# An instruction order for four engines, worked out in the kernel's source by an account of times, in the recurrence stage of a two-layer encoder

## The chip, the core and the metric

The kernel runs on one core of a Trainium2 chip. The metric is the device time of one execution in microseconds (us). A core has the engines PE (matrix products), DVE (VectorE), ACT (ScalarE) and POOL (GpSimd); SP issues most of the DMA loads. Each engine takes its instructions in the order in which the program holds them, and an instruction that waits for something holds up those behind it on the same engine. PEclk in a view is the clock that was granted to PE, as a share of full speed.

## The reference

Two layers over one sequence of 256 tokens of width 1024, all in fp32. Each layer has a token mixer and a mixture of experts, and each of these is modulated by shift, scale and gate rows that come from a conditioning vector `c`:

```python
for i in range(DEPTH):                               # DEPTH = 2
    mod = silu_c @ ada_w[i] + ada_b[i]
    sh_t, sc_t, ga_t, sh_c, sc_c, ga_c = jnp.split(mod, N_MOD, axis=-1)
    hn = modulate(rms_norm(x, norm_tm_g[i]), sh_t, sc_t)
    tm = rwkv7_mix(hn, ...) if i % 2 == 0 else dilated_attention_mix(hn, ...)
    x = x + ga_t[:, None, :] * tm
    hn = modulate(rms_norm(x, norm_cm_g[i]), sh_c, sc_c)
    x = x + ga_c[:, None, :] * hier_moe(hn, ...)
```

`rwkv7_mix` of layer 0 is a bidirectional delta-rule recurrence: `S_t = S_{t-1}(diag(w_t) + a_t^T b_t) + v_t^T k_t`, `y_t = S_t r_t`, for 16 heads of 64 and both directions, with low-rank projections for decay, rate and output gate, a norm over each head and an output product `o @ w_o`. `hier_moe` picks one of 4 groups and two of its 8 experts for each token; all 32 experts have weights to load.

## The kernel before, in words

The program has these stages in a row: the modulations that layer 0's mixer needs, the recurrence stage (65 to 451 us of the profiled execution), the choice of the experts, the experts of layer 0, the attention, the experts of layer 1.

**The recurrence stage** works on 8 pairs of heads. A pair i goes through: `project(i)` (products `kr` and `v` from 1 MB and 640 KB of weights, then `rates`), `scale_keys` and `chunks` (products `G`, `BT`, `R2`, done when `("ready", i)` is), `inverse(i)` (a chain of small fp16 products `iv`, each of which waits for a copy on ACT or DVE of the one before), `recur(i)` (four steps of products `R`, `U`, `S`, `Y`) and `finish(i)` (norm, transposition `yT`, gate, sum into `oT[:, i]`). `finish_last` ends pair 7: its last instruction writes `oT<-gsq,sT`, and it is called the last finish here. The output product `wo` goes over `oT` in two halves: 16 matmuls over pairs 0 to 3 (`out_first`), then 16 over pairs 4 to 7 (`out_second`), and its sums are added to `x`.

**The modulation flow.** Beside all this `modulation_flow` sums six more modulation rows (gate, shift and scale that the experts of layer 0 and the mixer of layer 1 need). Each row is a product of `silu(c)` with 1024 x 1024 weights, made on DVE: 8 chunks of 512 KB come by DMA into `aring`, two buffers, and each is multiplied and added to `acc` in two instructions of 512 columns. After the eighth chunk of a row, PE sums over partitions (tile `ada`), and DVE makes columns of it (`modc`, `nsh`, `nsc`). So there are 48 chunks and 96 adds. When all are done the flow marks `("ada", 0)`.

**What waits for `("ada", 0)`.** The generator `releases` gives the memory of the stage back part by part, each time followed by `later(n)`, which opens more buffers for the weights stream `wring`. Its first line is `yield after(("project", 7), ("ada", 0))`. Until then `wring` has two buffers. The router of the experts (`start_router`) waits for `("ada", 0)` too: its bias `lb` is a product with the modulation's shift.

**The weights stream.** All weights of the program come over one queue, SP, in a fixed plan: `kr` and `vl` (the `v` weights) of the 8 pairs, four loads `rwo` of 1 MB for `wo`, 96 of 1 MB for the experts of layer 0 (`wring<-in_w_moe_dram`), then those of the attention (`qkv`) and of layer 1's experts. The `rwo` weights are multiplied by the gate row on POOL before use. The `aring` loads stand on the same queue.

**What sets the order.** The function `weave` runs the generators of the stage, one step of one generator at a time. A step records its instructions, and a generator yields how many microseconds it would rest, or what it waits for (`after(...)`). In the kernel before, `weave` counts the PE work recorded so far as its clock, and takes among the ripe generators the one with the lowest `RANK`. PE's instructions then keep the order of recording; those of DVE, ACT, POOL and SP are ordered by a scheduler with the priority that `weave` sets from its clock and `OFFSET`:

```python
            ripe = [s for s in free if s[2] <= now]
            s = min(ripe, key=lambda v: RANK[v[1]]) if ripe else min(free, key=lambda v: v[2])
...
            tc.cur_priority = base + int(20 * max(0.0, 10 + now + OFFSET[s[1]]))
            r = next(s[0], "end")
```

PE's result banks are the pools `pp`, `ps`, `iv` and `ch`, two each. In `modulation_flow` a chunk is followed by `yield PACE` (4.0), and a whole row by 5.0 more.

## Time and profile before

| | us |
|---|---|
| median of three timed executions | 1194.64 |
| lowest and highest of them | 1184.44, 1194.68 |
| the profiled execution's own time | 1175.46 |
| its span in the trace | 1173.7 |
| PE busy in the span | 1031.4 (88%) |
| DVE busy | 620.2 (53%) |
| ACT busy | 431.6 (37%) |
| POOL busy | 149.7 (13%) |
| HBM read, mean over the span | 319.22 MB, 273 GB/s with what is written |

Busy time is the time in which an engine worked on an instruction; the shares are means over stages that differ much, so a stage is read by its own window. The profiled execution is below the timed ones; a difference worked out in its times is put on the median as it is.

### The profile page before, as it was taken

To read this page: it belongs to the slowest core of one execution; us is meant where nothing else is said; L and a number is where in the kernel's file an instruction comes from. 1 tells how busy PE (TensorE), PEld (TensorE's weight loads), DVE (VectorE), ACT (ScalarE), POOL (GpSimd) and SP (SyncE) were. 2 spreads that over 40 slices of the span, in tenths; PEclk is the share of its full clock that TensorE was granted. 3 is DMA by queue.
4 is the path that set the end of the run, shared out by engine and by line. 5 is a ranking of instruction groups with operands and counts; after the bars stand their busy time and mean duration, and the time that the engine had idled before them with its cause. 6 is when DMAs were issued, how large, how long until landed. Compare 5 with 4: busy or idle time off the path is not lost. (4 is left out here: it accounts for less than half of the span.)

```text
span 1173.7 us, 25024 instructions
## 1 busy us (share of the span) xinstructions
PE 1031.4 (88%) x10580; PEld 675.4 (58%) x10580; DVE 620.2 (53%) x1460; ACT 431.6 (37%) x913; POOL 149.7 (13%) x110
## 2 busy tenths in 40 slices
PE   7789889999988998978987899898979999789886
PEld 2666667766766555434442388687868754344422
DVE  4774678478585446212211367999984752121112
ACT  2544455455446342101000366656544621010012
POOL 1020010010012600000000012122472000000000
PEclk9789999899979999989998999999989999899999
DMA  9462524325243676998999987887745589999995
GB/s 366 179 237 77 181 77 151 109 95 168 74 131 129 269 288 251 388 418 358 421 420 421 420 358 266 310 303 275 282 145 171 209 339 409 413 370 421 420 422 234
DMA packets 53197, 322.01 MB, mean 274 GB/s; under 512 B 5922, under 2 KB 6562, under 8 KB 21458
## 3 DMA queue, kind: packets, MB, share of 16 engines
q1 hardware_dynamic: 51986, 315.88, 69.0%
q0 software_dynamic: 800, 3.36, 0.7%
q8 instruction: 87, 1.43, 0.5%
q10 hardware_dynamic: 288, 1.05, 0.3%
q14 instruction: 36, 0.29, 0.1%
HBM read 319.22 MB, written 1.05 MB: 273 GB/s over the span
## 5 line engine op out<-in xcount | busy, mean ns | idle before, releaser
L271 PE MATMUL gu<-wring,xT 128*32 128x512 f32 x1024 | 132.6, 616 | 16.8 <-PEq L1609 10.2
L376 DVE SCALAR_TENSOR_TENSOR acc<-aring,silu,acc 128x512 f32<-128x512 f32 x140 | 116.0, 860 | 17.5 <-DMA aring<-in_w_ada_dram 17.3
L467 POOL TENSOR_TENSOR wl<-wring,wh 128x1024 f16<-128x1024 f32 x24 | 57.0, 2377 | 403.4 <-ACT wh L466 400.9
L271 PE MATMUL qkv<-hh,wh 128*128 128x256 f16 x384 | 106.1, 276 | 1.8 <-ACT hh L1761 1.8
L271 PE MATMUL qkv<-hl,wh 128*128 128x256 f16 x384 | 105.7, 276 | 1.8 <-DVE hl L1762 1.8
L271 PE MATMUL qkv<-hh,wl 128*128 128x256 f16 x384 | 106.0, 276 | 1.2 <-DVE wl L473 1.2
L271 PEld LDWEIGHTS gu<-wring,xT 128*32 128x32 f32 x1024 | 30.8, 112 | 100.5 <-issue 82.0
L271 PEld LDWEIGHTS <-wh 128*128 128x128 f16 x768 | 76.1, 99 | 12.8 <-issue 3.5
L271 PE MATMUL dn<-wring,hidT 128*32 128x256 f32 x1024 | 65.5, 404 | 18.4 <-ACT hidT L1564 18.4
L473 DVE SCALAR_TENSOR_TENSOR wl<-wring,wh 128x1024 f16<-128x1024 f32 x56 | 70.5, 1264 | 16.4 <-ACT wh L469 16.3
L271 PE MATMUL acc<-y,back 128*128 128x512 f32 (+1 forms) x144 | 66.0, 581 | 10.3 <-DVE y L1591 8.1
L271 PEld LDWEIGHTS xT<-oh,x 128*128 128x128 f32 x512 | 59.0, 192 | 21.1 <-issue 9.2
L469 ACT ACTIVATE wh<-wring 128x1024 f16<-128x1024 f32 x56 | 58.6, 1050 | 33.0 <-PE qkv L271 23.2
L1366 DVE SCALAR_TENSOR_TENSOR sg<-sg,gu 128x256 f32<-128x256 f32 x16 | 6.7, 420 | 116.8 <-ACT sg L1365 116.8
L1591 DVE TENSOR_TENSOR y<-dn,ga 128x512 f32<-128x512 f32 x28 | 19.4, 692 | 88.3 <-PE dn L271 56.7
L271 PE MATMUL xT<-oh,x 128*128 128x128 f32 x512 | 63.5, 280 | 2.5 <-DVE oh L1475 2.5
L1365 ACT ACTIVATE sg<-gu 128x256 f32<-128x256 f32 x16 | 6.1, 384 | 145.6 <-PE gu L271 145.6
L271 PEld LDWEIGHTS dn<-wring,hidT 128*32 128x32 f32 x1024 | 31.9, 115 | 48.2 <-ACT hidT L1564 22.3
L1507 ACT ACTIVATE back<-bT 128x256 f32<-128x256 f32 x16 | 6.2, 386 | 131.0 <-PE acc L271 131.0
L271 PE MATMUL qkv<-wh,hh 128*128 128x256 f16 x192 | 52.3, 273 | 0.0
L271 PE MATMUL qkv<-wh,hl 128*128 128x256 f16 x192 | 52.3, 273 | 0.0
L271 PE MATMUL qkv<-wl,hh 128*128 128x256 f16 x192 | 52.3, 273 | 0.0
(355 smaller groups left out, 2090.4 us busy)
## 6 DMA issues: line engine op xcount, KB each, us to landing
wring<-in_w_moe_dram SPq DMA_DIRECT2D x192, 1024.0 KB, 19.8
aring<-in_w_ada_dram SPq DMA_DIRECT2D x96, 512.0 KB, 4.6
wring<-in_w_qkv_dram SPq DMA_DIRECT2D x36, 1024.0 KB, 8.4
wring<-in_w_kr_dram SPq DMA_DIRECT2D x8, 1024.0 KB, 5.9
wring<-in_w_vl_dram SPq DMA_DIRECT2D x8, 640.0 KB, 5.0
wring<-in_w_rwo_dram SPq DMA_DIRECT2D x4, 1024.0 KB, 8.1
wring<-in_w_ato_dram SPq DMA_DIRECT2D x4, 1024.0 KB, 6.6
x<-in_x_dram POOLq DMA_DIRECT2D x2, 512.0 KB, 7.2
```

The source lines that it names most:

```text
L271: return on_pe(nc.tensor.matmul(out=o, lhsT=lhsT, rhs=rhs, start=start, stop=stop, **kw))
L376: V.scalar_tensor_tensor(out=acc[:, s], in0=w[:, s], scalar=silu[:, k:k + 1], in1=acc[:, s], op0=ALU.mult, op1=ALU.add)
L467: eng.tensor_tensor(out=lo, in0=src, in1=hi, op=ALU.subtract)
L469: A.activation(out=hi, in_=src, func=AF.Copy, scale=by)
L473: V.scalar_tensor_tensor(out=lo, in0=src, scalar=by, in1=hi, op0=ALU.mult, op1=ALU.subtract)
L1365: A.activation(out=o, in_=ps[:, 0:256], func=AF.Tanh, scale=0.5)
L1366: V.scalar_tensor_tensor(out=o, in0=o, scalar=1.0, in1=ps[:, 0:256], op0=ALU.add, op1=ALU.mult)
L1507: A.activation(out=back, in_=ps[:, 0:S], func=AF.Copy)
L1591: V.tensor_tensor(out=y, in0=py[c], in1=gates[i, 5][:, c * 512:(c + 1) * 512], op=ALU.mult)
```

## The change

The order of the recurrence stage is now made in the source for PE, DVE, ACT and POOL. `account` keeps for each engine the time at which it is free, and for each tile when it was written and read; prices are in `COST` (a fixed part and one by element) and in `mm`, `HAND` is what a hand-over from one engine to another takes. An `Engine` wrapper around DVE, ACT and POOL prices each instruction and keeps it in program order. A generator now yields the engine of its next step and the tiles or bank pools that the step needs; `weave` works out when each live generator's next step could start, adds the stream's `GIVE_WAY`, and takes the smallest.

The steps are cut finer for this (a yield ahead of nearly each instruction), and some are moved: the results `Y` of the recurrence have a generator of their own (`results`) and a bank pool of their own (`ch=1, yy=1` in place of `ch=2`), `inverse(i)` waits for `("matrices", i)`, which is marked earlier than `("ready", i)`, `hidden_gate` runs as a generator of its own, two mixes of the token shift (`xv`, `xg`) are made by DVE and ACT step by step. The products are fp32 as before. `modulation_flow` has two accumulators of 512 columns, its adds are on DVE as before, and in the account a chunk's adds start no earlier than 6.0 after the end of the adds of the chunk before.

```diff
-RANK = dict(X=0, C=1, R=2, F=3, D=4, G=5, S=6, H=6, W=7, A=2.5)
-OFFSET = dict(X=0, C=-6, R=-4, F=-2, D=-2, G=-1, S=0, H=0, W=0, A=8)
+GIVE_WAY = dict(X=0, C=0, R=0, D=0.1, Y=0.2, F=0.3, G=0, K=0, S=0.1, B=0.3, H=0, W=0.5, A=0.3)
+
+COST = dict(V=(0.16, 0.00105), A=(0.19, 0.0008), P=(0.15, 0.00217))
+HAND = dict(T=0.3, V=0.15, A=0.15, P=0.15)
+SWITCH = 0.1
...
+    def account(e, t, outs, ins):
+
+        start = free[e]
+        for n in ins:
+            w = wrote.get(n)
+            if w:
+                start = max(start, w[0] + (0.0 if w[1] == e else HAND[w[1]]))
+        for n in outs:
+            w = wrote.get(n)
+            if w and w[1] != e:
+                start = max(start, w[0] + HAND[w[1]])
+        free[e] = end = start + t
+        for n in outs:
+            wrote[n] = (end, e)
+        for n in ins:
+            read[n] = max(end, read.get(n, 0.0))
+        step_end[0] = max(step_end[0], end + HAND[e])
+
...
+                        account(self.e, 0.1, [], [])
+                    else:
+                        a, b = COST[self.e]
+                        n = max(int(np.prod(v.shape[1:])) for v in outs)
...
-
-        return tc.keep_in_program_order(i) if pinned[0] else i
+            psum_n.pop()
+
+    def on_pe(i, o, a, b, t):
+        if pinned[0]:
+            tc.keep_in_program_order(i)
+            k = (a.shape[0] <= 64, int(np.prod(a.shape[1:])) <= 64, b.dtype)
+            if k != kind[0]:
+                t += SWITCH * (2 if b.dtype == F32 else 1)
+            kind[0] = k
+            account("T", t, [o.tensor.name], [a.tensor.name, b.tensor.name])
+        return i
...
     def weave(*streams):
 
 
-        live = [[g, n, 0.0, None] for g, n in streams]
+
+
+        live = [[g, n, 0.0, ("T", ())] for g, n in streams]
         base, now, pinned[0] = tc.cur_priority, 0.0, True
+        for t in (free, wrote, read, slots):
...
+            e, deps = s[3]
+            t = free[e]
+            for d in deps:
+                if isinstance(d, str):
+                    d = released(d)
+                    if d is None:
+                        return None
+                elif d is True:
+                    d = s[2]
+                elif not isinstance(d, float):
+                    w = wrote.get(d.tensor.name, (0.0, e))
+                    d = w[0] + (0.0 if w[1] == e else HAND[w[1]])
+                t = max(t, d)
+            return t
+
         while live:
+            best = None
...
-            free = [s for s in live if not s[3]]
-            assert free, [s[1] for s in live]
-            ripe = [s for s in free if s[2] <= now]
-            s = min(ripe, key=lambda v: RANK[v[1]]) if ripe else min(free, key=lambda v: v[2])
-            now = max(now, s[2])
-            before = pe_work[0]
-            tc.cur_priority = base + int(20 * max(0.0, 10 + now + OFFSET[s[1]]))
+                if callable(s[3]):
+                    if not s[3]():
+                        continue
+                    s[2], s[3] = max(s[2], now), ("T", ())
+                t = start_of(s)
+                if t is None:
+                    continue
+                v = t + GIVE_WAY[s[1]] - (SWITCH if s is last and s[3][0] == "T" else 0.0)
+                if best is None or v < best[0]:
+                    best = (v, t, s)
+            assert best, (now, [(s[1], s[3]) for s in live], {k: [(n, wrote.get(n), read.get(n)) for n in v[-3:]] for k, v in slots.items()})
+            _, now, s = best
+            step_end[0] = now
+            tc.cur_priority = base + int(20 * now)
             r = next(s[0], "end")
+            last = s
             if r == "end":
                 live.remove(s)
                 continue
-            used = pe_work[0] - before
-            now += used + (0.12 if used else 0.0)
...
-        ctx2.enter_context(banks(pp=2, ps=2, iv=2, ch=2))
+        ctx2.enter_context(banks(pp=2, ps=2, iv=2, ch=1, yy=1))
...
         def modulation_flow():
 
-            for i, m, k in ADA_RWKV:
+            taken = 0.0
+            for n, (i, m, k) in enumerate(ADA_RWKV):
                 w = modulations.take((i, m, k))
                 if k == 0:
-                    acc = modulations.pools[0][0].tile([128, D], F32, name="acc", tag="acc", bufs=1)
-                ada_add(acc, w, k, k == 0)
...
+                    g = gates[i, m] = const.tile([128, D], F32, name=f"ga{m}", tag=f"ga{m}", bufs=1)
+                    P.dma_start(out=g, in_=ap["p_adab"][i:i + 1, m * D:(m + 1) * D].to_broadcast([128, D]))
+                for e in range(2):
+                    yield ("V", taken + 6.0, PACE * n + 4.0)
+                    a, v = acc[e], w[:, e * 512:e * 512 + 512]
+                    if k == 0:
+                        V.tensor_scalar(out=a, in0=v, scalar1=silu[:, k:k + 1], scalar2=None, op0=ALU.mult)
+                    else:
+                        V.scalar_tensor_tensor(out=a, in0=v, scalar=silu[:, k:k + 1], in1=a, op0=ALU.mult, op1=ALU.add)
...
-        streams = dict(X=releases(), C=recurrences(), R=inverses(), F=finishes(), D=readies(), G=last_gates(),
-                       S=supply(), W=outputs(), A=modulation_flow())
+        streams = dict(X=releases(), C=recurrences(), R=inverses(), D=readies(), Y=results(), F=finishes(),
+                       G=last_gates(), S=supply(), B=hidden_gate(), W=outputs(), A=modulation_flow())
```

**Place 1: DVE around the last finish.** `oT<-gsq,sT` is the last finish, `acc` are the sums of the modulations, `x_64` and `x_65` the two halves of `x`. In the program before:

```order
L1187 TENSOR_TENSOR YT<-YT,rsy 128x2x128
L1194 TENSOR_TENSOR gsq<-yT,g_5961 128x256
L1195 TENSOR_TENSOR oT<-gsq,sT 128x256
L596 SCALAR_TENSOR_TENSOR x_64<-wo,x_64 128x512 x2
L596 SCALAR_TENSOR_TENSOR x_65<-wo,x_65 128x512 x2
L565 COPY zT<-zT 128x4x128
L496 TENSOR_REDUCE nss<-sums 128x2
```

In the changed program, from the same instruction on:

```order
L306 TENSOR_TENSOR gsq<-yT,g_6113 128x256
L306 TENSOR_TENSOR oT<-gsq,sT 128x256
L306 SCALAR_TENSOR_TENSOR acc_6143<-aring,silu,acc_6143 128x512
L306 SCALAR_TENSOR_TENSOR acc_6144<-aring,silu,acc_6144 128x512
L306 SCALAR_TENSOR_TENSOR acc_6143<-aring,silu,acc_6143 128x512
```

and behind these, when the pair of `acc` adds has stood there four times:

```order
L306 TENSOR_TENSOR modc<-ada,cols 128x8
L306 TENSOR_SCALAR nsh<-modc 128x8
L306 SCALAR_TENSOR_TENSOR x_64<-wo,x_64 128x512 x2
L306 TENSOR_SCALAR acc_6621<-aring,silu 128x512
L306 TENSOR_SCALAR acc_6622<-aring,silu 128x512
L306 SCALAR_TENSOR_TENSOR x_65<-wo,x_65 128x512
L306 SCALAR_TENSOR_TENSOR acc_6621<-aring,silu,acc_6621 128x512
L306 SCALAR_TENSOR_TENSOR acc_6622<-aring,silu,acc_6622 128x512
L306 SCALAR_TENSOR_TENSOR x_65<-wo,x_65 128x512
```

Before, no add into `acc` stands behind the last finish. In the changed program 24 of the 96 adds do, those of the last 12 chunks: four chunks of one row, then the eight of the next row, among which stand the adds of `wo` to `x` and the chain `nss` that makes the norm of `x`.

**Place 2: PE at the same point.** The last `yT` is what the last finish reads. Before:

```order
L271 MATMUL wo<-wring,oT 128x512 x4
L275 MATMUL yT<-cst,YT 128x128 x2
L271 MATMUL wo<-wring,oT 128x512 x5
L275 MATMUL zT<-cst,x_64 128x128 x8
L275 MATMUL zT<-cst,x_65 128x128 x4
L271 MATMUL lg<-rws,zT 128x36
L275 MATMUL zT<-cst,x_65 128x128 x4
```

Changed:

```order
L348 MATMUL wo<-wring,oT 128x512 x4
L352 MATMUL yT<-cst,YT 128x128 x2
L348 MATMUL wo<-wring,oT 128x512 x12
L348 MATMUL ada<-cst,acc_6143 128x1 x4
L348 MATMUL ada<-cst,acc_6144 128x1 x4
L348 MATMUL wo<-wring,oT 128x512 x4
L348 MATMUL ada<-cst,acc_6621 128x1 x4
L348 MATMUL ada<-cst,acc_6622 128x1 x4
L348 MATMUL lb<-rw_72,modc 1x36 x8
```

Behind the last `yT` there were 5 `wo` matmuls; now there are 16, with 16 `ada` and 8 `lb` among and behind them, ahead of the transpositions `zT` that the router starts from. The first 16 `wo` now end with the four ahead of `yT`. In the whole stage PE changes the kind of its work (tile shape or type of the weights) 373 times in place of 395, counted in the two orders.

**Place 3: SP from the last loads of `v` weights on.** Before:

```order
L153 DMA wring<-in_w_vl_dram 128x1280
L153 DMA aring<-in_w_ada_dram 128x1024 x4
L153 DMA wring<-in_w_kr_dram 128x2048
L153 DMA aring<-in_w_ada_dram 128x1024 x4
L153 DMA wring<-in_w_vl_dram 128x1280
L153 DMA aring<-in_w_ada_dram 128x1024 x2
L153 DMA wring<-in_w_rwo_dram 128x2048 x4
L153 DMA wring<-in_w_moe_dram 128x2048 x45
```

Changed, from the second `rwo` group on (the `aring` rows that follow alternate in the same way with `moe` rows up to 41 of the latter in a row):

```order
L156 DMA wring<-in_w_rwo_dram 128x2048
L156 DMA aring<-in_w_ada_dram 128x1024 x2
L156 DMA wring<-in_w_rwo_dram 128x2048
L156 DMA aring<-in_w_ada_dram 128x1024 x5
L156 DMA wring<-in_w_rwo_dram 128x2048
L156 DMA aring<-in_w_ada_dram 128x1024 x3
L156 DMA wring<-in_w_rwo_dram 128x2048
L156 DMA aring<-in_w_ada_dram 128x1024 x2
L156 DMA wring<-in_w_moe_dram 128x2048
L156 DMA aring<-in_w_ada_dram 128x1024 x2
L156 DMA wring<-in_w_moe_dram 128x2048
```

Before, all 48 loads into `aring` stood ahead of the first `rwo`, and the 96 expert loads of layer 0 followed with no `aring` between them. In the changed program 10 `aring` loads stand behind the fourth `rwo`, and only 4 expert loads ahead of the last `aring`; the fourth `rwo` takes the `wring` buffer of the second, which is read by the second 8 of the first 16 `wo`.

## Rows read from the trace of the kernel before

**Rows 1.** Busy time by engine in the recurrence stage and the first experts.
```profile
core 0: us, PE busy (x) PEld busy (x) DVE busy (x) ACT busy (x) POOL busy (x), PEclk, DMA share, GB/s
65.00:450.00 385.00, 349.86 (x5187) 255.63 (x5188) 244.88 (x631) 184.68 (x415) 56.88 (x46) 0.94 0.43 150
...
469.00:667.00 198.00, 171.69 (x1384) 76.74 (x1384) 40.33 (x99) 23.28 (x68) 0.00 (x0) 0.96 0.98 405
```

**Rows 2.** What PE waited for in 65 to 450 us: total, times, longest.
```profile
PE kr L271 <- ACT at L806: 4.9, 3, 1.7
PE R L271 <- DVE SD L1099: 4.3, 6, 1.1
PE yT L275 <- DVE rsq L352: 3.5, 2, 2.9
```

**Rows 3.** Two windows inside the recurrence stage, columns as in rows 1.
```profile
215.00:225.00 10.00, 10.00 (x86) 7.94 (x87) 4.65 (x13) 1.68 (x5) 0.00 (x0) 0.60 0.34 105
320.00:340.00 20.00, 16.66 (x189) 11.89 (x190) 15.19 (x43) 9.53 (x19) 2.43 (x2) 0.57 0.53 163
```

**Rows 4.** A window inside the first experts, columns as in rows 1.
```profile
560.00:580.00 20.00, 18.52 (x162) 8.92 (x163) 4.87 (x11) 2.55 (x7) 0.00 (x0) 1.00 1.01 421
```

**Rows 5.** SP's queue in time: start, length, loads in a row.
```profile
360.80 14.06 SPq L153 DMA_DIRECT2D wring<-in_w_rwo_dram  x4
374.90 87.04 SPq L153 DMA_DIRECT2D wring<-in_w_moe_dram  x22
...
596.05 47.55 SPq L153 DMA_DIRECT2D wring<-in_w_moe_dram  x20
```

**Rows 6.** The page's DMA issues: count, KB, median us to landing.
```profile
wring<-in_w_moe_dram SPq DMA_DIRECT2D x192, 1024.0 KB, 19.8
```

**Rows 7.** DMA issues of 60 to 360 us, as in rows 6.
```profile
aring<-in_w_ada_dram SPq DMA_DIRECT2D x44, 512.0 KB, 3.9
wring<-in_w_kr_dram SPq DMA_DIRECT2D x7, 1024.0 KB, 5.9
```

**Rows 8.** DVE in time: the last sums, the last finish, the first output sum.
```profile
347.55 2.07 DVE L376 SCALAR_TENSOR_TENSOR acc<-aring,silu,acc 128x512 f32<-128x512 f32 x3
...
450.82 0.42 DVE L1195 TENSOR_TENSOR oT<-gsq,sT 128x256 f32<-128x256 f32 x1
452.46 0.69 DVE L596 SCALAR_TENSOR_TENSOR x<-wo,x 128x512 f32<-128x512 f32 x1 [1.22 <-PE wo L271]
```

**Rows 9.** PE in time around the last finish (two records are one matmul).
```profile
449.92 0.41 PE L275 MATMUL yT<-cst,YT 128*128 128x128 f32 x2 [0.26 <-DVE YT L1187]
450.16 4.84 PE L271 MATMUL wo<-wring,oT 128*128 128x512 f32 x10
```

**Rows 10.** PE's groups in 65 to 450 us: records, busy, mean ns.
```profile
L271 PE MATMUL wo<-wring,oT 128*128 128x512 f32 x54 | 29.5, 645 | 1.8 <-DVE x L596 1.8
L271 PE MATMUL ada<-cst,acc 128*128 128x1 f32 x64 | 9.8, 283 | 0.0
L271 PE MATMUL lb<-rw,modc 128*1 128x36 f32 x16 | 0.7, 197 | 0.0
```

**Rows 11.** PE in time, `kr` matmuls alone between other kinds.
```profile
86.08 1.03 PE L271 MATMUL kr<-xk,wring 128*128 128x256 f32 x4
86.95 0.60 PE L275 MATMUL BT<-cst,BK 128*128 128x128 f32 x4
...
113.41 1.13 PE L271 MATMUL kr<-xk,wring 128*128 128x256 f32 x4
114.47 0.44 PE L271 MATMUL iv<-Q,X 64*64 64x64 f16 x16
```

**Rows 12.** DVE's sums of the modulations in 65 to 450 us, as in rows 10.
```profile
L376 DVE SCALAR_TENSOR_TENSOR acc<-aring,silu,acc 128x512 f32<-128x512 f32 x79 | 61.0, 792 | 14.2 <-DMA aring<-in_w_ada_dram 14.1
L374 DVE TENSOR_SCALAR acc<-aring,silu 128x512 f32<-128x512 f32 x10 | 4.6, 481 | 0.0
```

**Rows 13.** POOL's gating of the output weights in 65 to 450 us.
```profile
L590 POOL TENSOR_TENSOR wring<-wring,ga 128x512 f32<-128x512 f32 x16 | 20.2, 1291 | 12.9 <-PE R L271 12.9
```

More of the change, by code (lines that the diff above doesn't have):

```diff
@@ new lines, in trunk, with __init__, __getattr__, call @@
+    class Engine:
+        def __init__(self, e, nc_engine):
+            self.e, self.nc_engine = e, nc_engine
+        def __getattr__(self, name):
+            f = getattr(self.nc_engine, name)
+            def call(*args, **kw):
+                i = f(*args, **kw)
+                if pinned[0]:
+                    tc.keep_in_program_order(i)
+                    aps = [(k, v) for k, v in itertools.chain(enumerate(args), kw.items()) if hasattr(v, "tensor")]
+                    outs = [v for k, v in aps if k in ("out", "accum_out", 0)]
+                    ins = [v for k, v in aps if k not in ("out", "accum_out", 0)]
+                    if name == "dma_start":
+                        account(self.e, 0.1, [], [])
+                    else:
+                        a, b = COST[self.e]
+                        n = max(int(np.prod(v.shape[1:])) for v in outs)
+                        account(self.e, a + b * n, [v.tensor.name for v in outs], [v.tensor.name for v in ins])
+                return i
+            return call
@@ L787, in keys, with first_keys @@
             ws[i] = dict(sq=sq, kT=krT[:, 0], rT=krT[:, 1])
+        def first_keys():
+            kr = stream.take(("kr", 0)).rearrange("p (j k n) -> p j k n", j=2, k=KD)
+            ps = bank(name="kr", tag="pp")
+            for j, xs in enumerate((xk, xr)):
+                for _ in product(ps[:, j * S:(j + 1) * S], kr[:, j], xs):
+                    pass
+            keyed(0, ps, 1.0)
         def rates(i, w):
+            yield ("T", w["sq"], "pp")
             ps = bank(name="ss", tag="pp")
@@ L1173, in finish_last @@
         def finish_last(w):
-            yield after(("half", 7), ("gates", 0), ("finish", 6))
+            yield after(("early", 7), ("gates", 0), ("finish", 6))
             y4 = w["YT"].rearrange("p z a n -> p (z a) n")
@@ L1235, in out_first @@
         def out_first():
-            yield after(("project", 7), ("finish", 3), ("gate", 2))
             for c in range(2):
-                w = gated(stream.take(("rwo", 0, c)), gates[0, 2][:, c * 512:(c + 1) * 512], 4)
-                yield 6.0
+                w = stream.take(("rwo", 0, c))
+                yield from gating(w, gates[0, 2][:, c * 512:(c + 1) * 512], 4)
                 for t in range(NTT):
+                    yield ("T", w, oT, "pp")
                     ps = bank(name="wo", tag="pp")
@@ L1266, in outputs @@
+            for w in two:
+                yield from gating(w, gates[0, 2], 2)
+                blocks2.append(w.rearrange("p (k n) -> p k n", k=2))
+            yield after(("inverse", 7), ("finish", 5), ("finish", 6))
             for t in range(NTT):
                 for c in range(2):
+                    yield ("T", "iv" if c else "ps")
                     po[t, c] = bank(name="wo", tag="iv" if c else "ps")
-            yield from out_second(po, (4, 5), blocks[0])
-            yield after(("finish", 6))
@@ L1271, in outputs @@
-            yield 1.0
-            yield from out_second(po, (6,), last_rows[0])
-        last_rows = []
-        for _ in keys(0):
-            pass
+                    wrote.pop(po[t, c].tensor.name)
+            yield from out_second((4, 5, 6))
+        first_keys()
         hidden()
-        ws[0].update(vl=stream.take(("vl", 0)), wait=0.0)
+        vls[0] = stream.take(("vl", 0))
         for _ in rates(0, ws[0]):
             pass
-        done.add(("rates", 0))
-        xv = kept(2, "xv")
@@ L1312, in finishes @@
             for i in range(7):
-                yield after(("recur", i))
+                yield after(("outputs", i))
                 yield from finish(i, ws[i])
-            yield after(("half", 7))
+            yield after(("early", 7))
             yield from finish_last(ws[7])
@@ L1319, in start_router @@
             yield after(("ada", 0), ("recur", 6))
-            yield from router.start()
+            yield ("T", "pp")
+            for _ in router.start():
+                yield ("T", True)
         def releases():
```

471 lines of the change are left out of this document (302 added, 169 removed).

## The prediction

> **What bounds the kernel now.** I read the busy times by stage first. In the recurrence stage PE works 349.86 of 385 us and is the busiest engine by far, so only 35.1 us there are idle [rows 1]; the reader is to see that no order can take the stage below its PE work. In the first experts PE works 171.69 of 198 us, but the DMA share is 0.98 [rows 1], and a window in the middle has 1.01 and 421 GB/s [rows 4]: there the weights come no faster. 1 MB (1.0486 million bytes) at 421 GB/s is 2.49 us, while PE takes 171.69/96 = 1.79 us for what 1 MB brings. So the end of the first experts is set by when their loads start and how many are in by the time the experts begin. Then I read the queue of the loads: the four `rwo` loads start at 360.80, expert loads follow at 374.90 without a gap in the plan, 22 of them by 461.9, and the last is issued at 596.05 + 47.55 = 643.6 [rows 5]. With 19.8 us to landing [rows 6] it is in at 663.4. The last finish ends at 450.82 + 0.42 = 451.2 [rows 8]; I call this time F, and F' the same event in the changed program. So in the kernel before the expert weights are complete at F + 212.
>
> The stage and the loads have to be summed apart, because the change touches both, and in opposite directions.
>
> **Part 1: the order of the stage, F' against F.** Three terms make the last finish earlier.
>
> First, PE work that moves behind it. Behind the last `yT` stood 5 `wo` matmuls, now 16 (place 2). A record group of 54 is 27 matmuls in 29.5 us, so 1.09 us each [rows 10]: 11 x 1.09 = 12.0 us. 16 `ada` matmuls at 9.8/32 = 0.306 us are 4.9 us, and eight `lb`, half of 0.7 us and a little, about 1 us [rows 10]. Together 18 us no longer stand ahead of F'. This isn't a gain of the kernel, it is only later; it returns in part 2.
>
> Second, 22 fewer changes of kind on PE. The price of one is bounded by two places. A group of two `kr` matmuls between `BT` transpositions is followed 0.87 us after its start, the same group between `iv` products after 1.06 us [rows 11]. So a change costs 0 to about 0.2 us; I take 0.1, the middle, 2 us in all.
>
> Third, idle time. The waits that an account of the hand-overs can see coming are those in which PE's fixed order put a product at the head too early: `kr` for the copies of `rates` (4.9), `yT` for the norm chain (3.5) [rows 2]. I take these two, 8 us, as what the order saves: in the middle of the stage there is always another product to put there. `R` waits for `SD` inside the recurrence itself (4.3, six times) [rows 2]; at the end of the stage, where pair 7 has no pair behind it, nothing can fill that, so I leave it. The bounds: 6 us of idle more, when pinned DVE and ACT queues make the longest wait (2.9) [rows 2] come twice again, and 30 us less, when nearly all of the 35.1 vanishes.
>
> The clock is a fourth, which I set at nothing. In 215 to 225 and 320 to 340 us the granted clock was 0.60 and 0.57 while PE was busy in 10.0 of 10 and 16.66 of 20 us [rows 3], the lower of its two levels for most of that time. At full clock these 30 us would have taken 10 x 0.40 + 20 x 0.43 = 12.6 us less. The first window shows the low clock under full load, so nothing in these rows says that another order would avoid it.
>
> Sum: F' = F - (18 + 2 + 8) = F - 28. Bounds of this gain: 18 + 0 - 6 = 12, and 18 + 2 + 30 + 12.6 = 63.
>
> DVE gets 32 instructions for the two mixes and many small pinned ones; it is busy in 245 of 385 us [rows 1], so I cost them at nothing as long as the order lets them run beside PE's 350. If that cover is gone they are in the lower bound.
>
> **Part 2: the tail behind F'.** DVE holds 24 adds of the modulations behind the last finish (place 1), and SP holds 10 `aring` loads behind the fourth `rwo` (place 3). Before, the last adds ran at 347.55 to 349.6 [rows 8], 100 us ahead of the last finish. Followed step by step:
>
> The fourth `rwo` waits for the buffer that the second 8 `wo` read; these end just ahead of the last `yT`, and `yT` starts 1.3 us before F [rows 8, 9]. So it is issued at F' - 1.5. A 1 MB load landed after 5.9 us in this stage [rows 7]: F' + 4.4. POOL multiplies it in four pieces of 1.29 us [rows 13]: F' + 9.6. The 8 `wo` that don't need it are done by then, four that do run until F' + 14, and `ada` until F' + 16.4. Meanwhile chunks 38 and 39 have landed and are summed (two adds of 0.79 a chunk, 1.6 us) [rows 12], and 40 and 41 load into the two buffers. The last four `wo` end at F' + 20.8. DVE's order puts two sums into `x` (0.69 each [rows 8]) ahead of chunk 40, the other two and the norm chain ahead of chunk 42. So chunk 40 is summed at about F' + 21, 41 at F' + 23, and the adds of 42 start at about F' + 25. From here two buffers turn: a buffer that is freed is loaded 3.9 us later [rows 7], so two chunks take 3.9 + 1.6, about 5.5 us. The loads of 42 and 43 have been issued when 40 and 41 were summed, so they wait for DVE; chunks 42 to 43 end at F' + 28, 44 to 45 at F' + 34, 46 to 47 at F' + 39. The last `aring` load is issued when 45 is summed, at F' + 34.
>
> Behind it, and not earlier, SP issues the other 92 expert loads. SP's queue is in order, and the DMA queues idle meanwhile. 92 x 2.49 = 229 us: the weights are complete at F' + 34 + 229 = F' + 263, against F + 212 before. That is 51 us later from the last finish on. Without the sums of `wo` in DVE's order, five pairs of chunks would turn every 5.5 us from about F' + 3 on, and the last `aring` load would be issued at about F' + 25: 42 us later. I take 51 and keep 42 as the bound.
>
> The router waits for the last modulation too: `ada`, `lb`, then `zT`, at about F' + 42 where the first `x` sum came 1.2 us behind F [rows 8]. So the experts start about 39 us later from F'. From there PE needs 96 x 1.79 = 172 us, which ends ahead of the loads, so the loads are the later line. What follows (attention, second experts) starts that much later and is as long as before.
>
> In a sentence apart: the Trainium skill, DMA: Bandwidth & Descriptors, section "Where 436 GB/s comes from", says that loads from HBM are bound at about 358 GB/s for a core. By that 92 loads would take 269 us, and the sum would come out 40 us later. The trace disagrees with 421 GB/s in the window of [rows 4], and the measurement decides; as a case of its own I give it no chance.
>
> **The sum.** -28 + 51 = +23 us. The profiled execution took 1175.46 us, 1.8 over its span, so it would take 1198; the timed median was 1194.64, and I put the difference on that: 1217.6, rounded to 1218.
>
> **The rivals.**
>
> A, forecast: F' 18 to 38 us earlier, +13 to +33 in all.
>
> B, within 1%: the order takes most of the idle time away, F' 40 to 60 us earlier. With 22 us of idle less in place of 8, F' is 42 us earlier and the sum is +9: 1204. For it: the generator cuts are fine, and a product is nearly always at hand. Against it: the 35.1 us are spread over many waits of about 1 us [rows 2], and the steps of one pair's recurrence follow each other through DVE and ACT.
>
> C, faster, by an order without gaps: PE in the recurrence stage goes from one product to the next without idle time, and with the gaps both stretches of low clock vanish. Then F' is 63 us earlier and the tail costs 51, or 42 at its bound: -12 to -21, 1174 to 1183. It decides once the stage gains over 51, and by over 1% at 63. Against it: PE was busy all through the first of these stretches [rows 3].
>
> D, slower still, the account doesn't order the engines better than the scheduler did: its prices are fixed numbers, and a pinned DVE queue waits at its head where the scheduler let a later instruction pass in its plan. Then only the moved work remains, less new waits: F' 12 us earlier or not at all, +39 to +51: 1234 to 1246.
>
> **How the numbers follow.** A measurement of this kernel tells about 1% (12 us) from no change; the three times before lie 10 us apart. Chances: A 0.60, B 0.20, C 0.08, D 0.12. A and D are slower by over 1%, B is within 1%, C faster: 0.72, 0.20, 0.08. The range leaves out C and the upper half of D: 1186 to 1240. The predicted time is A's, 1218.
>
> **What would show it.** In the profile of the changed kernel: adds into `acc` on DVE for some 39 us behind `oT<-gsq,sT`; SP's first long row of expert loads starting some 34 us behind it; DMA in its rows of GB/s low at that point where it was high; the first experts with DMA near 1 and ending some 267 us behind the last finish; PE's idle in the stage about 27 us. The prediction is wrong if the last finish comes over 40 us earlier, if the `aring` loads run far ahead of their place on DVE so that expert loads aren't held, or if the first experts end by PE and not by the loads.

## The result, and the profile after

The changed kernel takes 1236.26 us in the median, the kernel before took 1193.18 beside it: a ratio of 1.0413 (95% interval 1.0375 to 1.0452), 43 us slower. The profiled execution took 1233.82 us. The forecast was slower by 23 us: right in direction and in the mechanism of the tail, about half the size.

Busy time by stage in the changed kernel, where the first window ends with the last finish, the second with the last sum of a modulation, and the third lies over the first experts (columns as in rows 1):

```profile
65.00:439.00 374.00, 330.83 (x5110) 244.66 (x5111) 250.97 (x621) 187.73 (x427) 53.03 (x45) 0.92 0.30 98
439.00:478.00 39.00, 18.00 (x52) 8.84 (x51) 23.28 (x42) 2.89 (x8) 5.83 (x4) 0.71 0.76 269
478.00:740.00 262.00, 211.55 (x1602) 105.17 (x1603) 66.17 (x180) 39.35 (x95) 4.21 (x2) 0.89 1.00 412
```

PE's work ahead of the last finish fell by 19 us against [rows 1], as the moved products say, but the window shrank by 11 only: the idle time in it grew from 35.1 to 43.2 us. The second window is new. PE does 18 us of work in 39, while all but four of the expert loads are held back. The prediction had the DMA queues idle there; they aren't: the last `rwo`, ten modulation loads and the four expert loads pass, at 269 GB/s and a DMA share of 0.76. Behind it the DMA share is 1.00; it was 0.98 in [rows 1].

DVE in time, in the changed kernel:

```profile
439.01 0.42 DVE L306 TENSOR_TENSOR oT<-gsq,sT 128x256 f32<-128x256 f32 x1
...
454.42 0.87 DVE L306 TENSOR_SCALAR acc<-aring,silu 128x512 f32<-128x512 f32 x2
...
456.13 1.40 DVE L306 SCALAR_TENSOR_TENSOR acc<-aring,silu,acc 128x512 f32<-128x512 f32 x2
...
474.77 2.74 DVE L306 SCALAR_TENSOR_TENSOR acc<-aring,silu,acc 128x512 f32<-128x512 f32 x4 [3.84 <-DMA aring<-in_w_ada_dram]
```

SP's queue in time, in the changed kernel:

```profile
437.94 0.33 SPq L156 DMA_DIRECT2D wring<-in_w_rwo_dram  x1
...
469.56 1.74 SPq L156 DMA_DIRECT2D aring<-in_w_ada_dram  x2
...
477.54 218.10 SPq L156 DMA_DIRECT2D wring<-in_w_moe_dram  x92
```

The last finish ends at 439.43 (F'), 11.8 us ahead of F in [rows 8]. The last sum ends at 477.51, and 92 expert loads begin at that moment, F' + 38, where 96 had begun at 374.90 in [rows 5]. They are in at 477.54 + 218.10 + 19.8 = 715.4, which is F' + 276 against F + 212. That is 64 us later from the last finish on, less 11.8: 52 us. The first product of the attention starts at 725.90 in place of 674.07, 52 us later. (The profiled executions lie 58 us apart and the medians 43, because the profiled one before was 1.5% below its median. Of the 58, 6 come behind that first product: 506.1 us from there to the end against 499.6, where e2_before_late, whose code there is that of the kernel before, took 506.4. No trace shows where the rest of the 1.5% lies, so against a median execution F' may be more than 11.8 us ahead of F.)

What PE waited for in 65 to 440 us in the changed kernel: total, times, longest:

```profile
PE iv L348 <- DVE X L306: 9.2, 3, 6.3
PE G L348 <- DVE AR L306: 6.6, 1, 6.6
PE R L348 <- DVE SD L306: 4.6, 7, 1.5
PE iv L348 <- DVE Q L306: 4.1, 6, 1.1
```

The waits that led [rows 2] (`kr`, and `yT` for the norm) are gone from the head of the list, as forecast. Two single waits of over 6 us are new, and both lie in the first 20 us of the stage.

### The profile page after: what moved, and what is told of

Its sections match the earlier page's. It is cut to its first block, busy times and chain, and to the rows that moved or that the text cites. A ratio compares the mean times of both kernels' runs of the same rounds, so it can differ in the third digit from the quotient of the medians.

```text
span 1232.0 us, 25037 instructions
## 1 busy us (share of the span) xinstructions
PE 1039.7 (84%) x10580; PEld 681.4 (55%) x10580; DVE 636.0 (52%) x1460; ACT 428.4 (35%) x913; POOL 143.3 (12%) x102
## 5 line engine op out<-in xcount | busy, mean ns | idle before, releaser
L306 DVE SCALAR_TENSOR_TENSOR acc<-aring,silu,acc 128x512 f32<-128x512 f32 x140 | 119.0, 890 | 14.6 <-DMA aring<-in_w_ada_dram 14.5
L306 ACT ACTIVATE wh<-wring 128x1024 f16<-128x1024 f32 x80 | 83.7, 1051 | 49.4 <-PE qkv L348 43.6
L348 PE MATMUL dn<-wring,hidT 128*32 128x256 f32 x1024 | 68.7, 418 | 17.4 <-ACT hidT L306 17.4
L306 DVE TENSOR_TENSOR y<-dn,ga 128x512 f32<-128x512 f32 (+1 forms) x36 | 22.8, 632 | 110.3 <-PE dn L348 66.6
L306 DVE SCALAR_TENSOR_TENSOR sg<-sg,gu 128x256 f32<-128x256 f32 x32 | 13.4, 418 | 107.0 <-ACT sg L306 106.6
L348 PEld LDWEIGHTS acc<-y,back 128*128 128x128 f32 x144 | 25.7, 196 | 60.8 <-DVE y L306 40.2
## 6 DMA issues: line engine op xcount, KB each, us to landing
wring<-in_w_moe_dram SPq DMA_DIRECT2D x192, 1024.0 KB, 19.8
```

The source lines that it names most:

```text
L306: i = f(*args, **kw)
L348: return on_pe(nc.tensor.matmul(out=o, lhsT=lhsT, rhs=rhs, start=start, stop=stop, **kw), o, lhsT, rhs, t)
```

## The experiments

Twelve kernels, in three groups: the tail, the loss inside the stage, and what else could be had. Ratios are to the kernel before, run on the same chip beside each; its median moved between 1185 and 1193 us from one series to the next, so ratios are compared, not times.

**The tail removed from the changed kernel (e1_mods_early).**

```diff
-GIVE_WAY = dict(X=0, C=0, R=0, D=0.1, Y=0.2, F=0.3, G=0, K=0, S=0.1, B=0.3, H=0, W=0.5, A=0.3)
+GIVE_WAY = dict(X=0, C=0, R=0, D=0.1, Y=0.2, F=0.3, G=0, K=0, S=0.1, B=0.3, H=0, W=0.5, A=-1.0)
```

> The changed kernel with one number other: the stream of the modulations gives way by -1.0 in place of 0.3, so that the order recorded puts all 96 adds ahead of the last finish and all loads of modulation weights ahead of the third load of output weights. Theory 1 (the tail): the 43 us come from the 10 loads of modulation weights behind the last finish, which hold 92 expert loads back. Then the last finish comes later by the 18 us of PE work that is put ahead of it again (about 457 us), the expert weights are complete some 212 us behind it as before, and the time is 1193 to 1206 us. Theory 2 (the order itself): the pinned order of four engines is what costs, and the late modulations only sit in time that is lost anyway. Then it stays over 1220 us.

Measured: 1.0153 (1.0107 to 1.0198), 1202.25 us. SP's queue in time in e1_mods_early:

```profile
353.92 307.68 SPq L156 DMA_DIRECT2D wring<-in_w_moe_dram  x96
```

The last finish on DVE in e1_mods_early:

```profile
463.59 0.43 DVE L306 TENSOR_TENSOR oT<-gsq,sT 128x256 f32<-128x256 f32 x1
```

All 96 expert loads now start 110 us ahead of the last finish, and are in at 681.4, F' + 217. From 1.0413 to 1.0153 is 2.6%, 31 us: the last finish comes 24.6 us later, the loads are complete 59 us sooner behind it, which makes 34. Theory 1 holds and theory 2 falls. But the last finish is 7 us later than the 457 expected, and 12.8 us later than in the kernel before, with 5.4 us less work ahead of it: 10 output products stand behind the last transposition, where 5 stood before. So something in the stage costs.

**The tail put into the kernel before (e2_before_late).**

```diff
-ADA_PARTS, PACE = (4, 4, 4, 4, 4, 4, 4, 4, 0), 4.0
+ADA_PARTS, PACE = (4, 4, 4, 4, 4, 4, 4, 4, 0), 8.0
```

> The kernel before with one number other: PACE 8.0 in place of 4.0, which moves the last modulation chunks behind the last finish (41 expert loads then stand behind the last modulation load, as in the changed kernel). PE alone is pinned, as before. Theory 1: the late modulations cost here too what they cost in the changed kernel: the last finish some 10 to 18 us earlier, the expert weights complete 250 to 276 us behind it in place of 212, and 1223 to 1243 us. Theory 2: without the pinned order nothing is lost: below 1205 us.

Measured: 1.035 (1.0307 to 1.0392), 1226.69 us, in the range of theory 1. The last finish on DVE in e2_before_late:

```profile
444.83 0.43 DVE L1195 TENSOR_TENSOR oT<-gsq,sT 128x256 f32<-128x256 f32 x1
```

SP's queue in time in e2_before_late:

```profile
467.44 217.77 SPq L153 DMA_DIRECT2D wring<-in_w_moe_dram  x92
```

The last finish comes 6 us earlier, less than the 10 to 18 expected. 92 loads start 22 us behind it and are complete at 705.0, 260 us behind it, in the range of theory 1. Late modulations alone, with the old `weave`, cost 3.5%.

**The start of the stage (e6_early_mix).** The window of the first 30 us shows where the stage lost. The kernel before:

```profile
65.00:95.00 30.00, 27.00 (x193) 22.05 (x194) 18.51 (x43) 9.61 (x19) 2.75 (x2) 0.89 0.56 193
```

The changed kernel:

```profile
65.00:95.00 30.00, 17.72 (x196) 14.04 (x196) 20.38 (x51) 13.88 (x27) 3.58 (x4) 0.66 0.32 106
```

PE was busy 9.3 us less, and at a granted clock of 0.66 in place of 0.89. What DVE did there, in the changed kernel:

```profile
69.00 0.68 DVE L306 TENSOR_TENSOR AR<-krT,eb 128x512 f32<-128x512 f32 x1
69.60 1.66 DVE L306 SCALAR_TENSOR_TENSOR xv<-xx,muh,hT 128x256 f32<-128x256 f32 x4
...
76.49 1.76 DVE L306 SCALAR_TENSOR_TENSOR xv<-xx,muh,hT 128x256 f32<-128x256 f32 x2
78.18 1.11 DVE L306 SCALAR_TENSOR_TENSOR end<-muh,modc 128x8 f32<-128x8 f32 x1
79.22 1.66 DVE L306 SCALAR_TENSOR_TENSOR pBT<-xx,muh,hT 128x256 f32<-128x256 f32 x4
...
81.25 0.42 DVE L306 TENSOR_TENSOR X<-Ah,cst 128x512 f16<-128x512 f16 x1
```

PE beside it, in the changed kernel:

```profile
69.74 2.08 PE L348 MATMUL G<-AR,BK 64*128 64x128 f32 x16 [6.61 <-DVE AR L306]
73.08 2.37 PE L348 MATMUL G<-AR,BK 64*128 64x128 f32 x16 [1.26 <-DVE GI L306]
81.73 0.63 PE L348 MATMUL iv<-cst,X 64*64 64x64 f16 x16 [6.28 <-DVE X L306]
82.29 2.07 PE L348 MATMUL v<-xv,wring 128*128 128x256 f32 x4
```

PE in the kernel before:

```profile
65.07 2.86 PE L271 MATMUL v<-xv,wring 128*128 128x256 f32 x12 [0.51 <-ACT at L806]
...
77.76 8.05 PE L271 MATMUL hg<-pBT,wring 128*128 128x256 f32 x32
```

DVE's instruction `X` in the kernel before:

```profile
83.17 0.42 DVE L1010 TENSOR_TENSOR X<-Ah,cst 128x512 f16<-128x512 f16 x1
```

The mixes `xv` and `pBT` (the latter is `xg`) stand on DVE between the matrices and `X`, which starts the first inverse. They don't make `X` late: it starts at 81.25, and at 83.17 in the kernel before. What is lost is PE's work ahead of it: the products `v` and `hg`, which ran there before, are those that wait for the mixes, and now stand behind the first `iv`. e6_early_mix is e1_mods_early with both mixes ahead of `weave`, as the kernel before has them:

```diff
-            yield from passing_steps(2, t)
...
-            yield from passing_steps(5, t)
...
+        xv.extend(kept(2, "xv"))
+        xg = passing(5, "BT")
         router = Router(0, "pp") if "moe0" in stages else None
```

> As e1_mods_early, and the two mixes of the token shift (xv, xg) made ahead of the interleaved stage, as in the kernel before. Theory 3 (the start): in the changed kernel 16 adds of the mixes stand on DVE between the instructions that the first matrices and the first inverse wait for; PE was busy 17.7 of the first 30 us at a clock of 0.66 there, against 27.0 at 0.89 before, some 12 us of work. Then this is 8 to 13 us faster than e1_mods_early. If the mixes only move (PE then waits for the same chain a little earlier), it is within 4 us of it.

Measured: 0.9992 (0.9966 to 1.0018), 1185.92 us: 1.6% under e1_mods_early, or 16 us by the medians, somewhat more than theory 3 gave. The window in e6_early_mix:

```profile
65.00:95.00 30.00, 28.63 (x327) 23.47 (x327) 17.42 (x35) 10.95 (x22) 3.61 (x3) 1.00 0.54 198
```

The last finish in e6_early_mix:

```profile
446.47 0.43 DVE L306 TENSOR_TENSOR oT<-gsq,sT 128x256 f32<-128x256 f32 x1
```

PE behind its last transposition in e6_early_mix (two records are one matmul):

```profile
445.81 8.75 PE L348 MATMUL wo<-wring,oT 128*128 128x512 f32 x20
```

PE is busy 28.6 of 30 us at full clock, though `X` starts no earlier (83.58). The last finish is 17 us earlier than in e1_mods_early, with the same 10 output products behind the last transposition. It is 4.3 us earlier than before, which is less than the five products more that stand behind it are worth (5.4 us).

**The mixes alone taken out of the changed kernel (e5_mix_first)**, with the diff of e6_early_mix on the changed kernel:

> The changed kernel with the two mixes ahead of the stage and nothing else (30 adds of the modulations stand behind the last finish in place of 24). Theory 3 says that the mixes cost some 16 us in the changed kernel as they did in e1_mods_early, and theory 1 that each further chunk behind the last finish costs 2.8 us of the loads' start: 16 less and 3 x 2.8 = 8 more, about 8 us below the changed kernel, 1.030 to 1.039 of the kernel before. If the two costs don't add up, it is as slow as the changed kernel (1.041) or 16 us faster (1.027).

Measured: 1.0321 (1.0272 to 1.037), 0.9% under the changed kernel, 11 us where about 8 were expected. The last finish is 13 us earlier (426.3), and the 92 loads start at 468.0, 41.7 us behind it in place of 38.1. So what is won at the start is partly lost to three more chunks in the tail, as far as one pair of kernels tells.

**The pins (e7_early_pe).** e1_mods_early without the line that keeps DVE, ACT and POOL in the recorded order:

```diff
                 if pinned[0]:
-                    tc.keep_in_program_order(i)
```

> As e1_mods_early, but DVE, ACT and POOL aren't kept in the recorded order: the account still makes PE's order and the priorities. Theory 4: the pinned queues of the three engines make PE wait at their heads; then this is 5 to 15 us faster than e1_mods_early. Rival: pinning is what makes PE's order hold; then it is 5 to 20 us slower, with more idle time of PE in the stage.

Measured: 1.025 (1.0206 to 1.0293), 1.0% slower than e1_mods_early, 14 us by the medians. So theory 4 is wrong and its rival right: with PE in the account's order, pinning the other three engines pays. Busy time in e7_early_pe, then in e1_mods_early, for 65 to 430 us:

```profile
65.00:430.00 365.00, 308.23 (x4390) 234.34 (x4392) 231.84 (x546) 158.06 (x352) 49.26 (x40) 0.86 0.35 122
```

```profile
65.00:430.00 365.00, 315.11 (x4874) 238.94 (x4876) 249.31 (x597) 179.94 (x400) 43.65 (x38) 0.91 0.40 137
```

PE got through 4390 records in place of 4874. The first 30 us of e7_early_pe add something on theory 3:

```profile
65.00:95.00 30.00, 17.84 (x229) 13.68 (x230) 16.20 (x36) 8.43 (x17) 2.29 (x2) 0.66 0.47 168
```

Here DVE, free in its order, has made both mixes by 64 us, and PE is as idle as in the changed kernel: its own pinned order still has the first `v` behind the first `iv`, at 82.84. So, as far as this run tells, the loss at the start isn't DVE's time for the mixes; it is the place that PE's order gives to the products that read them.

**What else the order lacks (e8_gate_stream, e9_gate_dve, e10_pace55).** In e6_early_mix PE waited 4.4 us for the norm of pair 6. e8_gate_stream gates all output weights as soon as it can and lets products of pairs 4 and 5 run earlier:

```diff
+        def gatings():
+            yield after(("project", 7), ("gate", 2), ("later", 0))
+            gated4.extend(stream.take(("rwo", 0, 0), ("rwo", 0, 1), ("rwo", 1, 0), ("rwo", 1, 1)))
+            for n, w in enumerate(gated4):
...
-            yield after(("inverse", 7), ("finish", 5), ("finish", 6))
+            yield after(("inverse", 7), ("finish", 5), ("gated", 3))
```

> As e6_early_mix, with the gating of the output weights in a stream of its own that starts as soon as the gate row is there, and the output products of pairs 4 and 5 no longer held by finish 6 for the first half of the tokens. In e6_early_mix PE waited 4.4 us for the norm of pair 6 near the end with no product at hand, and 10 output products stood behind the last transposition against 5 before. Theory 5: what the order still lacks is work to fill in at the end; then this is 3 to 6 us faster than e6_early_mix. Rival: the gating on POOL now runs as one stretch of 20 us beside DVE and slows DVE's instructions there (in e6_early_mix single ones took 1.19 us in place of 0.16 while POOL gated); then it is as fast as e6_early_mix or slower.

Measured: 1.0057 (1.0034 to 1.0081), slower than e6_early_mix; its rival was right. POOL in time in e8_gate_stream:

```profile
339.90 23.33 POOL L306 TENSOR_TENSOR wring<-wring,ga 128x512 f32<-128x512 f32 x16 [0.48 <-PE Y L348]
```

DVE beside it, in e8_gate_stream:

```profile
347.86 1.19 DVE L306 SCALAR_TENSOR_TENSOR rsy<-rsq,rsy 128x4 f32<-128x4 f32 x1
349.08 1.19 DVE L306 TENSOR_TENSOR rsq<-rsy 128x4 f32<-128x4 f32 x1
...
352.64 1.83 DVE L306 TENSOR_TENSOR kd<-kd,krT 128x512 f32<-128x512 f32 x1
```

PE behind it, in e8_gate_stream:

```profile
357.92 0.69 PE L348 MATMUL R<-SD,AR 128*64 128x128 f32 x4 [6.01 <-DVE SD L306]
```

While POOL gates, DVE's instructions on 4 columns take 1.19 us, which take 0.16 elsewhere, and PE waits 6.0 us for a state `SD` behind them. e9_gate_dve puts the same 16 products on DVE:

```diff
-                    yield ("P", gate)
-                    P.tensor_tensor(out=wk[:, j, s], in0=wk[:, j, s], in1=gate[:, s], op=ALU.mult)
+                    yield ("V", gate)
+                    V.tensor_tensor(out=wk[:, j, s], in0=wk[:, j, s], in1=gate[:, s], op=ALU.mult)
```

> As e8_gate_stream, with the 16 gating products on DVE in place of POOL. Theory 6: DVE is held up while POOL gates, for up to 16 x 1.29 = 21 us in the stage, and that is worth more than the 16 x 0.7 = 11 us which DVE gets in work; then 3 to 8 us faster than e8_gate_stream, with no small DVE instruction above 0.3 us. Rival: DVE is too full at the end of the stage for 11 us more: 5 to 12 us slower.

Measured: 0.9999 (0.9974 to 1.0024), 0.6% or 7 us under e8_gate_stream, as theory 6 gave. The theory also had no small DVE instruction above 0.3 us, and that failed: four on 4 or 8 columns took 1.0 to 1.3 us, at 262 to 264 and 375 to 378 us, beside other products of POOL. DVE's products, by group, in e9_gate_dve:

```profile
L306 DVE TENSOR_TENSOR wring<-wring,ga 128x512 f32<-128x512 f32 x16 | 9.7, 685 | 0.0
```

e10_pace55 is e8_gate_stream with one other number, `taken + 5.5` for `taken + 6.0`:

> As e8_gate_stream, with the modulation chunks 5.5 in place of 6.0 apart in the account. The order of all four engines comes out another one, with the same work. If such an order's quality hangs on small differences in the prices, it lies anywhere within 10 us of e8_gate_stream; if the account's own end time is a good guide, 4 to 8 us below it, since the account ends the last finish 6 us earlier.

Measured: 0.9987 (0.996 to 1.0014), 0.7% or 8 us under e8_gate_stream. Both of its readings fit, and the next group tells them apart.

**No gating at all, and one price (e12_gate_sum, e13_gate_sum55, e14_scan_price, e15_scan_price55).** In e12_gate_sum the gate multiplies the sums of `wo`:

```diff
+        def gated_out(ps, c):
+            V.tensor_tensor(out=ps, in0=ps, in1=gates[0, 2][:, c * 512:(c + 1) * 512], op=ALU.mult)
...
-                yield from gating(w, gates[0, 2][:, c * 512:(c + 1) * 512], 4)
...
                     yield ("V", ps)
+                    gated_out(ps, c)
                     add_out(ps, t, c)
```

> As e6_early_mix, without the 16 gating products on the output weights: the gate row multiplies the 8 sums of wo instead, on DVE, ahead of each sum into x (the result is the same up to rounding). POOL then does no gating. Theory 6 (DVE stands still while POOL gates): in e6_early_mix PE waited 6.1 us for one state SD while POOL gated, and POOL gated for 20 us in the stage; with that gone the last finish is 6 to 12 us earlier, the tail some 3 us longer by four multiplications, and the time 3 to 9 us below e6_early_mix. Rival: the stalls beside POOL lay in DVE's slack but for that one; then within 3 us of it, or up to 3 us slower by the tail.

Measured: 0.9971 (0.9944 to 0.9998). The interval overlaps that of e6_early_mix, so the time tells no gain over it. The trace does show the stall gone: DVE in time in e12_gate_sum, the same chain as above:

```profile
342.21 0.16 DVE L306 SCALAR_TENSOR_TENSOR rsy<-rsq,rsy 128x4 f32<-128x4 f32 x1
342.41 0.16 DVE L306 TENSOR_TENSOR rsq<-rsy 128x4 f32<-128x4 f32 x1
```

> As e12_gate_sum, with the chunks 5.5 in place of 6.0 apart in the account and the first half of the tokens' output products not held by finish 6. 5 output products stand behind the last transposition in place of 10, so the experts start some 5 us earlier after the last finish, which itself comes 2 us later by the account: 2 to 5 us below e12_gate_sum. Rival: an order with other prices lies anywhere within 8 us of it, as e10_pace55 and e8_gate_stream do.

Measured: 0.997 (0.9949 to 0.9992), the same as e12_gate_sum within the intervals, not 2 to 5 us below it. The account had the last finish 2 us later than in e12_gate_sum; it came 12.7 us later (449.4 against 436.7). So the account's own end time, the second reading of e10_pace55, is no good guide here. Then one price of the account was set right:

```diff
-                        n = max(int(np.prod(v.shape[1:])) for v in outs)
+                        n = max(int(np.prod(v.shape[1:])) for v in outs) * (2 if name == "tensor_tensor_scan" else 1)
```

> As e12_gate_sum, with the two scans of each pair priced in the account at what they take (0.64 us where the account has 0.43). 4 output products stand behind the last transposition in place of 10. If mispriced instructions are what makes PE wait for DVE in the stage, the waits of PE for DVE (Q, SD, X, R: 22.6 us in e12_gate_sum) shrink and it is 4 to 10 us faster. If such a price matters no more than any other small shift of the order, within 8 us of it on either side.

Measured: 1.0034 (1.0008 to 1.0059), 0.6% slower than e12_gate_sum, though PE's waits for DVE's `Q`, `SD`, `X` and `R` did shrink, from 22.6 to 18.3 us.

> As e13_gate_sum55, with the same price of the scans. The account ends its last finish 5 us earlier than for e13_gate_sum55, but 12 output products stand behind the last transposition in place of 5 (some 7 us). Better prices: 2 to 6 us faster than e13_gate_sum55; otherwise within 8 us on either side.

Measured: 0.991 (0.9877 to 0.9944), 1175.62 us, 0.6% or 7 us faster than e13_gate_sum55, a little over the 2 to 6 expected of better prices, and the fastest of all kernels here. The last finish on DVE in e15_scan_price55:

```profile
434.87 0.42 DVE L306 TENSOR_TENSOR oT<-gsq,sT 128x256 f32<-128x256 f32 x1
```

The first product of the attention on PE in e15_scan_price55:

```profile
668.67 0.37 PE L348 MATMUL qkv<-hh,wh 128*128 128x256 f16 x1 [1.59 <-ACT hh L306]
```

They come 16 and 5 us earlier than in the kernel before. Of the difference, 5.6 us go to the 12 output products behind the last transposition in place of 5 (the router's first `zT` starts at 444.51, in place of 454.84), and about as much between this `zT` and the first product of the experts (463.88, in place of 469.05).

The same correct price made one order slower by 0.6% and the other faster by 0.6%. So a step of this size is no proof of a better price; small shifts of the order gave as much here. A version exists that is 0.9% faster than the kernel before, but which of its edits to e6_early_mix (the gate on the sums, the hold on the output products, the spacing, the price) it owes that to is not shown.

## Why the prediction was right in direction and half in size

**What bounds the kernel** held: the first experts follow the loads, at a DMA share of 1.00, and the stage behind them starts later by what the loads' end comes later, 52 us both.

**Part 1, F' = F - 28: measured F - 11.8, the lower bound of 12.** The terms for moved work and kinds fit (20 forecast, PE's work fell by 19). The idle time went the wrong way: 8 us less forecast, 8 more measured. In the first 30 us it grew by 9.3 (12.3 against 3.0); in the rest of the stage it fell by 1.2. The step that failed is the sentence that costs DVE's new instructions for the mixes at nothing "as long as the order lets them run beside PE's 350". That cover isn't there at the start of the stage, because the products that could have filled PE's time are those that wait for the mixes. e6_early_mix against e1_mods_early prices it at 1.6%, 16 us by the medians; e5_mix_first shows 13 us at the last finish of the changed kernel itself, and 0.9% in all. I read DVE's load from the mean of the whole stage (245 of 385 us), where PE's order in the first 30 us was to be read: DVE isn't full there either (20.4 of 30 us). The idle term failed with it: the two waits that I took for it did go, but others came in their place. e6_early_mix, without the loss at the start, shows no gain from idle time and kinds at its last finish, where the two terms said 10: it comes 4.3 us earlier, with 5.4 us less work ahead of it. That much can be chance: e12_gate_sum and e14_scan_price, one price apart, have their last finishes 15 us apart, and e13_gate_sum55 and e15_scan_price55 too. (The eight `lb` are the whole of their 0.7 us row [rows 10] and not half of it, which changes nothing.)

**The clock, set at nothing**, was part of that loss: the granted clock was 0.66 in the first window, with PE idle for 12.3 of 30 us, and 1.00 with 1.4 idle in e6_early_mix. The stretches of low clock under load [rows 3] gave no sign of this, and it went against the change, not for it.

**Part 2, loads complete at F' + 263: measured F' + 276.** The chain of steps was right to the first of them (the fourth `rwo` is issued at 437.94, F' - 1.5 as forecast) and to the last (sums of the last chunk end at F' + 38, forecast F' + 39). That its end fits so well is partly luck: the second chunk of the last row is summed at F' + 18, where F' + 23 was forecast, and the three pairs behind it take 6.7 us each, where 5.5 was. Two terms were too small. The 92 loads start at F' + 38 and not F' + 34: the next expert load stands behind the last `aring` load on SP, issued by 471.3, but begins only at 477.54, 0.03 us behind the last sum. In 470 to 480 us the profile puts SP's waits down to the landing of an `aring` load (4.7 us) and then to DVE's sums (2.5 in two waits), and `releases` gives the memory of `aring` to the expert weights; no run tried them apart. And they took 237.9 us and not 229, with a DMA share of 1.00 but 412 GB/s on the mean of the window in place of 421. Together 13 us; the 28 that became 11.8 is 16 more. By these the traces differ by 52 us where +23 was forecast; the medians differ by 43, for the reason given with the result. The 13 us are read from the changed kernel's trace against its forecast; of the 16, some may come from the fast execution of the kernel before, from which F is taken.

**The rivals.** The time is that of D (+39 to +51), but D's reason isn't what happened: pinning DVE, ACT and POOL gains 1.0% (e7_early_pe), and with the mixes and the tail as they were before, the account's order is as fast as the scheduler's (e6_early_mix, 0.9992). B and C needed a stage that gains over 40 us, and no order here came near: the best last finish with the modulations ahead of it starts at 434.87, 16 us ahead of that in [rows 8], and e5_mix_first, with more work behind it, has its own 25 us ahead.

In short, the 4.1% of the changed kernel are the tail, 2.6% (e1_mods_early), and then the mixes, 1.6% (e6_early_mix); taken out in the other order they are 0.9% (e5_mix_first) and 3.3%. What is left, the pinned order itself, is worth about nothing against the old one (0.9992), and 0.9% in the best of its variants (e15_scan_price55, 0.991). As orders one number apart lie some 0.6% apart, these sizes are good to about that; that both causes are there is shown by the loads' start and by the first window.

## What to carry to other kernels

When a new order is read for what it brings on the busiest engine, look at what it leaves for the end: a load queue that waits for the last piece of a side task delays the later stage that is bound by its loads (here the last load came 52 us later). A new instruction on an engine with slack is free only where its consumer isn't the filler that hides it; check the window, at the start and at the end of a stage above all, not the mean, and read there what the busiest engine still has to do. And orders that a planner makes from fixed prices differed here by some 0.6% at a change of one number, so a planner's parameters are compared by timing several orders, not by one.

## What the runs showed of the hardware that I had not expected

DVE is held up beside POOL's products. In e8_gate_stream, while POOL multiplied 16 tiles of 128x512 in a row, one every 1.46 us, DVE instructions on 4 columns took 1.19 us in place of 0.16, and `kd` and `bb`, on 512 columns, 1.83 and 1.74 in place of 0.68 and 0.69. The Trainium skill, SBUF — State Buffer, section "SBUF: two separate sides", says that a DVE instruction with two SBUF inputs (or in a two-port mode) and a GpSimd instruction that reads SBUF take a pair of ports that they share for a whole instruction each, and that the other is blocked. The trace agrees, with these numbers: the instructions on 4 columns are about 1.0 us longer, of the 1.46 of a product of POOL; the same chain takes 0.16 us an instruction in e12_gate_sum, where POOL does not gate.

The mean granted clock, which lies between the levels of 1.2 and 2.4 GHz, fell with PE's idle time at the start of the stage: 0.66 over 30 us in which PE was busy for 17.7, 0.60 in e1_mods_early with 16.6, and 1.00 in e6_early_mix with 28.6. A low clock also came without idle time: in the first window of [rows 3] it was 0.60 with PE busy throughout.
